# High and low parts of seven half rows of y moved into the staging tile of the output weights, at 14 address offsets

## The chip, the cores and the metric

The kernel runs on one core of a Trainium2 chip. A core has five engines with a queue each: TensorE (PE in the profile; its weight loads are shown apart, as PEld), VectorE (DVE), ScalarE (ACT), GpSimd (POOL) and SyncE (SP), which issues most DMAs. The metric is the time of one execution on the device in microseconds, taken as the median of several runs. All memory named below is the core's SBUF, 128 partitions wide; an address or a distance is counted in bytes within a partition.

## The reference

One layer of an encoder on a sequence of 1024 rows and 1024 channels, in float32:

```python
h = rmsnorm(x, norm_mix_w[l]) * (1 + sc_m) + sh_m
z, xbc, dt_raw, q, k, v = jnp.split(h @ w_in[l], IN_SPLITS, axis=-1)
y_ssd = ssd_mixer(z, xbc, dt_raw, ...)      # Mamba-2 scan, 512 columns
y_att = chunk_attention(q, k, v, rel_bias[l])   # 512 columns
x = x + g_m * (jnp.concatenate([y_ssd, y_att], axis=-1) @ w_out[l])
h = rmsnorm(x, norm_ffn_w[l]) * (1 + sc_f) + sh_f
x = x + g_f * conv_ffn(h, w_up[l], ffn_conv_w[l], w_down[l])
return rmsnorm(x, final_norm_w)
```

The change touches the line with `w_out`: y, 1024 by 1024, times the output weights.

## The kernel before

Matmuls are made from a faster float32 format (F32R). Each operand is split into a high part, which is the value rounded to that format, and a low part, the rest; a product is three matmuls: high by high, high by low, low by high. `split` (L88 to L94) does it in two instructions: L93 writes the high part, in the output projection on ScalarE, and L94 writes the low part on VectorE as value minus high part.

The work runs in stages: projections and attention (to about 250 us), the convolution and the z projection (to about 407 us), the scan with the output projection (about 407 to 540 us), the feed-forward up products (a Strassen-like scheme with tiles named uX, uY and uZ) and the down products (dn).

In the scan stage the sequence is cut into eight chunks c of 128 rows. Per chunk the scan computes `ydp`, `yop` and `stp` on TensorE, then on VectorE the sums `yy` (L1005 to L1008), the multiplication by the gate `zs` (L1013), a norm, and a transpose back into the tile `xs` (L1023, on ScalarE). GpSimd does part of the elementwise work. Between these pieces stands the output projection, which fills TensorE: row tile st (128 rows) of y is two half rows, `n = 2 * st + part`. Even n are the attention half, held in the tile `ya`; odd n are the scan's half, in `xs`. `wout_half(n)` (L1048) runs the 24 matmuls of half row n: for two column halves of the result and four blocks of 128 channels, three matmuls each. The y block (128 columns) is the stationary operand, that is, the weight load; the output weights (512 columns), kept in the tiles hH and hL, are the moving operand. The results gather in PSUM tiles named `wops`. When both halves of a row tile are done, `wout_row` adds the residual (L1080, L1081), stores it and computes the norm's sum.

`wout_rhs` (L1043) splits a half row ahead of its use: half row n + 1 is split when half row n begins. The target is the tile `yhl` with the tag `wh` in the pool `wu`: two buffers of 4096 bytes, used in turn, so that a split must wait until the matmuls of the half row that last used the buffer have read it. The same two buffers serve earlier stages, and later the feed-forward tiles `cv`. The remaining half rows, 9 to 15, are split after the scan, among the transposes of the feed-forward input.

`wos` (L690) is a tile of 3 x 1024 floats (12288 bytes) in the pool `bcp`. It stages the adaptive weights and the output weights while they are folded and split (L749, L760, L762); after the z projection it isn't used again. When the scan is over, `bcp` is closed (`es_b.close()`), and tiles of the feed-forward stage are laid over its memory, among them the tiles `a`, which are first written at L1179, and the tile `cg`.

In the kernel's allocation every large tile starts at the same address modulo 512 (448), the output weights and both buffers of `yhl` included. The z weight tiles are the exception: 2 x 288 floats (2304 bytes), two blocks of 1152 bytes, of which 260 floats are used.

The order of the work: on TensorE the instructions of the scan and of half rows up to 8 are tied one behind another by `pe` (L862). A few instructions on the other engines are tied to one another (`issue_after`). All else is placed on its engine by a planner that simulates the program, with the waits for buffers, when the program is built. From half row 14 (TensorE) and row tile 6 (VectorE, ScalarE) on, the order is that of the program's text (recorded under L66).

Of the kernel before, what the change touches and what calls it, by code (L numbers as in the profile page):

```python
# [10 lines left out]
F32 = mybir.dt.float32  # L11
F32R = mybir.dt.float32r
# [4 lines left out]
P = 128  # L17
D = 1024
# [20 lines left out]
XM = (5, 7, 7, 7)  # L39
WARM = (8, 26)  # L40
KH = NF // 2

B_ADA, NMIX, NFFN, SNW, SCW, SCB, FCW, DTB, ALOG, DSK = (
    0, 48, 56, 64, 68, 100, 108, 240, 248, 256)
# [4 lines left out]
def f32(ap):  # L49
    return ap.bitcast(F32)  # L50
# [22 lines left out]
def tile_block(ctx: ExitStack, tc: tile.TileContext, x, ccol, pk, w_ada, w_first, w_ft, w_z,  # L73
               w_out, w_up, w_down, bias, fnw, out, dbg=None):
    nc = tc.nc
    V, A, T = (InOrder(tc, e) for e in (nc.vector, nc.scalar, nc.tensor))
# [11 lines left out]
    def split(hi, lo, src, ehi, elo, scale=None):  # L88
        if scale is not None:
            A.activation(hi, src, AF.Copy, scale=scale)  # L90
            V.scalar_tensor_tensor(lo, src, scale, f32(hi), op0=ALU.mult, op1=ALU.subtract)
            return
        i = A.activation(hi, src, AF.Copy) if ehi is A else ehi.tensor_copy(hi, src)  # L93
        return i, elo.tensor_tensor(lo, src, f32(hi), ALU.subtract)  # L94
# [5 lines left out]
    wu = es_l.enter_context(tc.tile_pool(name="wu", bufs=2, reuse_waits="tile"))  # L100
# [38 lines left out]
    def raw_tile(n=1024):  # L139
        rawc[0] += 1  # L140
        return raws[:, rawc[0] % 2, 0:n]
# [34 lines left out]
    def c4(ap):  # L176
        return ap.rearrange("p (a b) -> p a b", a=4)
# [33 lines left out]
    def mod_shift(dst, sh, kt, n=1):  # L211
        return V.tensor_tensor(dst[:, kt:kt + n], modc[:, sh + kt:sh + kt + n],
                        pkt[:, B_ADA + sh + kt:B_ADA + sh + kt + n], ALU.add)
# [147 lines left out]
    for j in range(2):  # L361
        k = slice(4 * j, 4 * j + 4)
# [43 lines left out]
    for hh in range(2):  # L406
# [13 lines left out]
        for kt in range(KT):  # L420
            if hh == 0:
# [7 lines left out]
                t = raw_tile(768)  # L429
# [194 lines left out]
    def gemm_part(p, which, hhs):  # L624
        if which == 0:
            new_pair(p)
        if which == 2 and hhs == H1:
            wh, wl = held.pop(p)
        elif p == 2 and which < 2:
            with tc.issue_after(wpin[0].ins), tc.issue_after(wpin[1].ins):  # L630
                wh, wl = wu_pair(w_ft[8 + 3 * (p - 2) + which], A, V)
        else:
            wh, wl = wu_pair(w_ft[8 + 3 * (p - 2) + which], A, G)
        if which == 2 and hhs == H0:
            held[p] = wh, wl
        outs = {hh: psv.tile([P, 512], F32, tag="acc", bufs=1, name="acc") for hh in hhs}
        gemm_ft(wh, wl, outs, GPIN.get((p, which, hhs), {}), hhs)
        for hh in hhs:
            tmp = tps = None
            if which == 2:  # L640
                tmp, tps = p_tile()[:, 0:512], tp_tile()
            evac_qkv(p, which, hh, outs[hh], tmp, tps)
# [15 lines left out]
    part = lambda *a: (lambda: gemm_part(*a))  # L658
# [9 lines left out]
    x1 = (ya, xs)  # L668
# [9 lines left out]
    bcp = es_b.enter_context(tc.tile_pool(name="bcp", bufs=1, side="right", reuse_waits="tile"))  # L678
# [8 lines left out]
    tle1 = bcp.tile([P, 2, P], F32, name="tle1")  # L687
    tle, ones = tle1[:, 0, :], tle1[:, 1, :]
    sgt = bcp.tile([P, P], F32, name="sgt")
    wos = bcp.tile([P, 3, D], F32, name="wos")  # L690
    es_t = ExitStack()
    es_g = ExitStack()
    gm1 = es_g.enter_context(tc.tile_pool(name="gmp", bufs=1, side="left")).tile([P, 512], F32, name="gm1")
# [166 lines left out]
    def pe(op, *a, **k):  # L860
        with tc.issue_after(chain[0]) if chain and chain[0] else ExitStack():
            i = op(*a, **k)  # L862
        if chain:
            chain[0] = i.ins
# [161 lines left out]
    x1d = dram.tile([S, D], F32, name="x1d")  # L1026
    NM = (KH + 1) // 2

    def kn(m):
        return min(2, KH - 2 * m)  # L1030

    gd = {}
    for m in range(NM):
        for n, names in (("x", ("b11",)), ("y", ("t1", "t3")), ("z", ("t2", "t4", "b21", "b22"))):
            t = gd[n, m] = dram.tile([kn(m), P, len(names), 512], F32, name=f"g{n}{m}")
# [2 lines left out]

    mod_scale(affn, SC_F, NFFN, 0, KT)
    mod_shift(bffn, SH_F, 0, KT)  # L1040
    xr_, yq, wps, xrs = {}, {}, {}, []

    def wout_rhs(st, part):  # L1043
        if st < NT:
            y = yq[st, part] = wu.tile([P, 2, 4, P], F32R, tag="wh", name="yhl")
            return split(y[:, 0], y[:, 1], x1[part][:, st, :].rearrange("p (a b) -> p a b", a=4), A, V)[1].ins

    def wout_half(n, ks=slice(0, 8), fill=()):  # L1048
        st, part = n // 2, n % 2
        if ks.start == 0:  # L1050
            if part == 0:
                if not xrs:
                    xrs.append(wu.tile([P, 2, 2, 512], F32, tag="w2", bufs=1, name="xr"))
                xr_[st] = xrs[0][:, st % 2]
                nc.sync.dma_start(xr_[st].rearrange("p a b -> p (a b)"), x[st * P:(st + 1) * P, :])
                wps[st] = []
            for q in {0: (0, 2), 1: (), 2: ()}.get(n, (n + 1,)):
                wout_rhs(q // 2, q % 2)
        y = yq[st, part]
        for dh, k in [(dh, k) for dh in range(2) for k in range(4)][ks]:  # L1060
            w = ws[dh][4 * part + k]
            if len(wps[st]) <= dh:
                wps[st].append(ps2a.tile([P, 512], F32, tag="w1", bufs=1, name="wops") if n == 2 and not dh else
                               ps2b.tile([P, 512], F32, tag="wo", bufs=PB[0], name="wops"))
            ps = wps[st][dh]
            f, l = part == 0 and k == 0, part == 1 and k == 3
            pe(T.matmul, ps, y[:, 0, k, :], w[0], start=f, stop=False)
            pe(T.matmul, ps, y[:, 0, k, :], w[1], start=False, stop=False)
            pe(T.matmul, ps, y[:, 1, k, :], w[0], start=False, stop=l)
        if part == 1 and ks.stop == 8:  # L1070
            wout_row(st, *fill)

    def wout_row(st, mid=(), end=()):
        xr = xr_.pop(st)
        m = [stat(), stat()]
        for dh in range(2):
            src = wps[st][dh]
            if dh:
                src = x1[dh][:, st, :]
                V.tensor_tensor(src, wps[st][dh], gm1, ALU.mult)  # L1080
            V.tensor_tensor(xr[:, dh, :], src, xr[:, dh, :], ALU.add)  # L1081
            nc.scalar.dma_start(x1d[st * P:(st + 1) * P, halves[dh]], xr[:, dh, :])
            A.activation(x1[dh][:, st, :], xr[:, dh, :], AF.Square, scale=1.0 / 32.0, accum_out=m[dh])
        for fn in mid:
            fn()
        scale_[:] = [(st, xr, rstd2(m))]
        for fn in end:
            fn()
        if not chain:
            row_scale()  # L1090
# [22 lines left out]
    for c in range(NT):  # L1113
        if c == 1:
            ssd_turn(*turn)
        y, t = ssd_y(c, *pre)
        if c > 1:
            ssd_turn(*turn)
        if c == 1:
            at = wout_rhs(0, 1)  # L1120
        if c == 2:
            wout_half(2, slice(4, 8))
            wout_rhs(1, 1)
        if c > 1:
            ssd_norm(c, y, t)
        turn = (c, y)
        n, k = ((0, slice(0, 3)), (2, slice(0, 4)), (3, slice(0, 3)))[c] if c < 3 else (c + 1, slice(0, 3))
        if c < NT - 1:
            if c == 0:
                ssd_norm(c, y, t)  # L1130
            pre = ssd_pre(c + 1, x_tile, lambda: wout_half(n, k))
            late = pin[1]
            if c == 1:
                ssd_norm(c, y, t, at)
            row_scale(pin[0])
            if c == 1:
                wout_half(1)
            else:
                wout_half(n, slice(3, 8))
        else:  # L1140
            wout_half(c + 1)
# [42 lines left out]
    def a_tile():  # L1184
        return hp.tile([P, 2, S], F32, tag="a", bufs=2, name="a")
# [32 lines left out]
    class Unit:  # L1218
        def __init__(self, i):
            self.i, self.b, self.ps, self.w, self.done = i, (ya, xs)[i // KH], {}, {}, set()  # L1220
            nc.sync.dma_start(self.b[:, 0, :], w_up[i, :, 0, :])
            nc.sync.dma_start(self.b[:, 1:4, :], w_up[i, :, 1:4, :])
# [32 lines left out]
        def post(self, p):  # L1255
# [15 lines left out]
            elif p == "Q4":  # L1271
                V.tensor_tensor(self.v[:, 0:512], ps, self.v[:, 0:512], ALU.subtract)
                self.a = a_tile() if self.i % KH < KH - 1 else \
                    self.b[:, 0:4, :].rearrange("p (a b) c -> p a (b c)", a=2)
# [13 lines left out]
        def finish(self):  # L1288
# [3 lines left out]
            V.tensor_tensor(a[:, 1, :], a[:, 0, :], a[:, 1, :], ALU.mult)  # L1292
            if self.i < KH:
                nc.scalar.dma_start(gd["x", self.i // 2][self.i % 2, :, 0], a[:, 1, 0:512])
# [29 lines left out]
    for sts in ((0, 1), (2, 3)):  # L1324
# [4 lines left out]
        for n in (9,) if sts[0] == 0 else (10, 11):  # L1329
            wout_half(n)  # L1330
    units = [Unit(0), Unit(KH)]
    for u in units:
# [99 lines left out]
    bufs = {}  # L1432
# [317 lines left out]
```

## Time and profile before

| | |
|---|---|
| median of 3 runs | 1180.53 us (1179.7 to 1180.82) |
| the profiled execution | 1180.9 us |
| its span, first to last instruction | 1179.2 us |
| mean granted TensorE clock | 0.997 |
| PE busy | 1154.7 us (98%), 5839 matmuls |
| output projection | 384 matmuls of 512 columns, from 409.7 to 537 us |

In the views, a row such as "L862 PE MATMUL wops<-hH,yhl" names the source line, the engine, the operation and the tiles: written, then read. In a row of the timeline the first two numbers are the start and the duration in us; brackets at the end tell how long the engine sat idle before it and what ended that. In the view of instructions by tile the three numbers are the shortest, the median and the longest duration in ns. Matmuls overlap: one of 512 columns shows 389 ns, while the next one starts 227 ns later; starts tell the pace.

### The profile page before, as it was taken

How to read it: one execution, taken by the hardware profiler on the slowest of the kernel's cores; microseconds unless marked ns; L12 is line 12 of the kernel's file. 1: busy time of each engine (PE TensorE's matmuls, PEld its weight loads, DVE VectorE, ACT ScalarE, POOL GpSimd, SP SyncE). 2: the span in 40 equal slices, each digit the busy share in tenths (PEclk: the TensorE clock that was granted, in tenths of full speed). 3: DMA queues.
4: the chain of work that ended last, by engine and by line, in shares of the span. 5: the costliest groups of instructions: out<-in, count | busy, mean ns of one | idle time of the engine just before them, and what ended most of it. 6: DMA issues, size and time to landing. Idle time of an engine off the chain costs nothing.

```text
span 1179.2 us, 15793 instructions
## 1 busy us (share of the span) xinstructions
PE 1154.7 (98%) x5839; PEld 974.9 (83%) x5839; DVE 907.4 (77%) x1357; ACT 587.9 (50%) x971; POOL 162.2 (14%) x179
## 2 busy tenths in 40 slices
PE   8999999999999999999999999999999999999996
PEld 7778888888889988887788888888888888888885
DVE  7746465787676778558999988898888869666986
ACT  5636464674335665587444454434433445433454
POOL 1103343350000165200000000000000000000622
PEclk9999999999999999999999999999999999999999
DMA  9736344244558622141233222332233378633444
GB/s 349 260 83 158 100 121 125 57 153 128 185 179 294 224 101 81 64 152 36 95 110 134 101 80 95 128 127 75 93 107 116 117 277 301 242 122 121 160 134 152
DMA packets 63741, 169.15 MB, mean 143 GB/s; under 512 B 6880, under 2 KB 7344, under 8 KB 62256
## 3 DMA queue, kind: packets, MB, share of 16 engines
q1 hardware_dynamic: 56320, 143.11, 36.8%
q10 hardware_dynamic: 7344, 25.04, 5.4%
q8 instruction: 46, 0.75, 0.3%
q14 instruction: 31, 0.25, 0.1%
HBM read 125.87 MB, written 32.81 MB: 135 GB/s over the span
## 4 chain that ended last, share of the span: by engine, by line
PE 82%; DVE 11%; ACT 3%; issue 3%; POOL 1%; POOLq 0%; DVEq 0%; ACTq 0%
PE wops L862 5%; PE dn L86 5%; PE dn L84 5%; PE dn L85 5%; PE uY L86 5%; PE uY L84 5%; PE uY L85 5%; PE uX L86 3%; PE uZ L84 3%; PE uZ L85 3%; PE uZ L86 3%; PE uX L84 3%; PE uX L85 3%; PE s L84 3%; PE s L86 3%
## 5 line engine op out<-in xcount | busy, mean ns | idle before, releaser
L85 PE MATMUL dn<-w 128*128 128x512 f32 x296 | 107.4, 389 | 0.0
L84 PE MATMUL dn<-w 128*128 128x512 f32 x296 | 107.4, 389 | 0.0
L86 PE MATMUL dn<-w 128*128 128x512 f32 x296 | 99.9, 390 | 0.1
L84 PE MATMUL uY<-tH,w 128*128 128x512 f32 x248 | 96.5, 389 | 0.0
L86 PE MATMUL uY<-tH,w 128*128 128x512 f32 x248 | 96.5, 389 | 0.0
L85 PE MATMUL uY<-tL,w 128*128 128x512 f32 x248 | 96.5, 389 | 0.0
L1611 POOL TENSOR_TENSOR ya<-ya,xs 128x512 f32<-128x512 f32 x4 | 18.2, 4590 | 551.0 <-ACT xs L1607 551.0
L93 ACT ACTIVATE w<-ya 128x1024 fp32r<-128x1024 f32 (+1 forms) x41 | 39.2, 955 | 85.2 <-PE uY L86 75.2
L862 PE MATMUL wops<-hH,yhl 128*128 128x512 f32 x224 | 73.0, 397 | 0.6 <-DVE yhl L94 0.6
L535 POOL TENSOR_SCALAR p<-p,st 128x640 f32<-128x640 f32 (+4 forms) x64 | 50.2, 794 | 116.4 <-DVE st L534 113.5
L86 PEld LDWEIGHTS dn<-w 128*128 128x128 f32 x296 | 55.4, 188 | 12.6 <-DVE w L94 1.2
L85 PEld LDWEIGHTS dn<-w 128*128 128x128 f32 x296 | 55.6, 188 | 11.6
L84 PEld LDWEIGHTS dn<-w 128*128 128x128 f32 x296 | 55.6, 188 | 11.5
L93 ACT ACTIVATE w<-xs 128x1024 fp32r<-128x1024 f32 (+1 forms) x41 | 39.2, 955 | 37.1 <-PE uY L86 30.9
L529 DVE CUSTOM_DVE_ANT_0 p<-s,bias 128x640 f32<-128x640 f32 (+4 forms) x58 | 38.3, 675 | 23.1 <-PE tp L561 8.8
L86 PEld LDWEIGHTS uY<-tH,w 128*128 128x128 f32 x248 | 46.5, 188 | 9.7
L84 PEld LDWEIGHTS uY<-tH,w 128*128 128x128 f32 x248 | 46.5, 188 | 9.7
L85 PEld LDWEIGHTS uY<-tL,w 128*128 128x128 f32 x248 | 46.6, 188 | 9.6
L532 ACT ACTIVATE p<-p,st 128x640 f32<-128x640 f32 (+4 forms) x64 | 44.1, 692 | 17.9 <-DVE st L529 17.4
L94 DVE TENSOR_TENSOR pt<-tp,pt 128x512 fp32r<-128x512 f32 (+2 forms) x72 | 41.8, 596 | 13.3 <-ACT pt L93 12.9
L1285 DVE SCALAR_TENSOR_TENSOR a<-cv,pkt,a 128x1023 f32<-128x1023 f32 (+1 forms) x40 | 51.1, 1280 | 0.1
L84 PE MATMUL s<-hH,wh 128*128 128x512 f32 x128 | 50.4, 394 | 0.1
(503 smaller groups left out, 3399.3 us busy)
## 6 DMA issues: line engine op xcount, KB each, us to landing
gz<-a ACTq DMA_DIRECT2D x10, 1024.0 KB, 5.1
ya<-in_w_up_dram SPq DMA_DIRECT2D x11, 768.0 KB, 4.2
xs<-in_w_up_dram SPq DMA_DIRECT2D x11, 768.0 KB, 4.2
adat<-in_w_ada_dram SPq DMA_DIRECT2D x16, 512.0 KB, 6.0
xs<-in_w_ada_dram SPq DMA_DIRECT2D x16, 512.0 KB, 4.8
raws<-in_w_ft_dram SPq DMA_DIRECT2D x15, 512.0 KB, 3.7
qk<-qk SPq DMA_DIRECT2D x56, 128.0 KB, 2.4
gy<-a ACTq DMA_DIRECT2D x10, 512.0 KB, 2.6
```

The costliest lines, as they stand in the source:

```text
L84: T.matmul(ps, lh, rh, start=start, stop=False, skip_group_check=more)
L85: T.matmul(ps, lh, rl, start=False, stop=False, skip_group_check=more)
L86: T.matmul(ps, ll, rh, start=False, stop=stop, skip_group_check=more)
L93: i = A.activation(hi, src, AF.Copy) if ehi is A else ehi.tensor_copy(hi, src)
L94: return i, elo.tensor_tensor(lo, src, f32(hi), ALU.subtract)
L529: V.tensor_tensor_reduce(out=dst, in0=src, in1=bsl, scale=-1.0, scalar=3e38, op0=ALU.add, op1=ALU.min, accum_out=nm)
L532: A.activation(pv_, pv_, AF.Exp, scale=-1.0, bias=nm, accum_out=rs)
L535: last_g.append(G.tensor_scalar(pv_, pv_, rr, 1.0, op0=ALU.mult, op1=ALU.mult).ins)
L862: i = op(*a, **k)
L1285: V.scalar_tensor_tensor(a[:, j:S], c[:, 0:S - j], w[2 - j], a[:, j:S], op0=ALU.mult, op1=ALU.add)
L1611: G.tensor_tensor(src, src, fnr[:, halves[1]], ALU.mult)
```

## The change

Seven half rows, n = 1 and 3 to 8, are no longer split into the two `wh` buffers but into a new tile `yhw`, which takes the memory of `wos` (tag "wos", one buffer, 2 x 1536 floats, again 12288 bytes). Its first half serves the even n and its second half the odd n. In each half the high part starts at `YOFF[n][0]` bytes and the low part at 2560 bytes plus `YOFF[n][1]` bytes. 2560 and the half's 6144 are multiples of 512, so these 14 numbers, from 16 to 496, are the distances modulo 512 from the output weights that the matmuls stream. Half rows 0, 2 and 9 to 15 stay in the `wh` buffers, which they now use in another turn. What is computed, and with which instructions, stays the same.

```diff
+YBASE = 0
+YOFF = {1: (256, 224), 3: (32, 288), 4: (192, 16), 5: (480, 240), 6: (320, 352), 7: (96, 416), 8: (160, 496)}
...
-    wos = bcp.tile([P, 3, D], F32, name="wos")
+    wos = bcp.tile([P, 3, D], F32, tag="wos", bufs=1, name="wos")
...
     def wout_rhs(st, part):
         if st < NT:
-            y = yq[st, part] = wu.tile([P, 2, 4, P], F32R, tag="wh", name="yhl")
-            return split(y[:, 0], y[:, 1], x1[part][:, st, :].rearrange("p (a b) -> p a b", a=4), A, V)[1].ins
+            n = 2 * st + part
+            if n in YOFF:
+                if not yh2:
+                    yh2.append(bcp.tile([P, 2, 3 * D // 2], F32R, tag="wos", bufs=1, name="yhw"))
+                t = yh2[0][:, n % 2, :]
+                y = [c4(t[:, o:o + 512]) for o in (YBASE + YOFF[n][0] // 4, YBASE + 640 + YOFF[n][1] // 4)]
+            else:
+                t = wu.tile([P, 2, 4, P], F32R, tag="wh", name="yhl")
+                y = [t[:, 0], t[:, 1]]
+            yq[st, part] = y
+            return split(y[0], y[1], c4(x1[part][:, st, :]), A, V)[1].ins
...
-            pe(T.matmul, ps, y[:, 0, k, :], w[0], start=f, stop=False)
-            pe(T.matmul, ps, y[:, 0, k, :], w[1], start=False, stop=False)
-            pe(T.matmul, ps, y[:, 1, k, :], w[0], start=False, stop=l)
+            pe(T.matmul, ps, y[0][:, k, :], w[0], start=f, stop=False)
+            pe(T.matmul, ps, y[0][:, k, :], w[1], start=False, stop=False)
+            pe(T.matmul, ps, y[1][:, k, :], w[0], start=False, stop=l)
```

More of the change, by code (lines that the diff above doesn't have):

```diff
@@ L1040, in tile_block @@
     mod_shift(bffn, SH_F, 0, KT)
-    xr_, yq, wps, xrs = {}, {}, {}, []
+    xr_, yq, wps, xrs, yh2 = {}, {}, {}, [], []
     def wout_rhs(st, part):
         if st < NT:
-            y = yq[st, part] = wu.tile([P, 2, 4, P], F32R, tag="wh", name="yhl")
-            return split(y[:, 0], y[:, 1], x1[part][:, st, :].rearrange("p (a b) -> p a b", a=4), A, V)[1].ins
+            n = 2 * st + part
[9 more added lines that the diff above has]
+            return split(y[0], y[1], c4(x1[part][:, st, :]), A, V)[1].ins
     def wout_half(n, ks=slice(0, 8), fill=()):
```

## The prediction

> **What bounds the kernel now.** I read the page first, then the busy time by stretches, then the waits of the stage that the change touches, then the chain and the timeline there.
>
> ```profile
> span 1179.2 us, 15793 instructions
> PE 1154.7 (98%) x5839; PEld 974.9 (83%) x5839; DVE 907.4 (77%) x1357; ACT 587.9 (50%) x971; POOL 162.2 (14%) x179
> L862 PE MATMUL wops<-hH,yhl 128*128 128x512 f32 x224 | 73.0, 397 | 0.6 <-DVE yhl L94 0.6
> ```
>
> TensorE is the bound: 98% busy, and the output projection (wops) lost only 0.6 us waiting for a split half row (yhl). Seven of the sixteen half rows move. The stretches of that stage (columns: PE, PEld, DVE, ACT and POOL busy, granted clock, DMA share, GB/s):
>
> ```profile
> 410.00:430.00 20.00, 20.00 (x110) 17.02 (x108) 13.32 (x17) 13.44 (x37) 13.69 (x14) 1.00 0.32 120
> 430.00:450.00 20.00, 19.41 (x106) 16.50 (x105) 17.24 (x23) 13.39 (x33) 11.35 (x12) 1.00 0.33 118
> 450.00:470.00 20.00, 19.74 (x115) 17.09 (x114) 17.10 (x24) 13.02 (x34) 11.22 (x12) 1.00 0.23 80
> 470.00:500.00 30.00, 29.80 (x160) 25.52 (x159) 18.31 (x28) 14.70 (x30) 8.78 (x11) 1.00 0.18 62
> ```
>
> PE is idle for 0 + 0.59 + 0.26 + 0.20 = 1.05 us in these 90 us, at the full clock. All that could be won here without faster matmuls is that 1.05 us. Who waited for whom between 406 and 545 us (total, times, longest):
>
> ```profile
> ACT yhl L93 <- PE wops L862: 0.6, 2, 0.4
> PE wops L862 <- DVE yhl L94: 0.6, 1, 0.6
> PE ydp L862 <- DVE th L908: 0.5, 2, 0.3
> ```
>
> The first row is the whole price of the two staging buffers: a split that has to wait until the matmuls of an older half row have read the buffer. It is 0.6 us, on ACT, not on PE. The second row is the one place where PE waits for a split. Its place in the chain, and on the engines:
>
> ```profile
> 434.73 0.69 DVE yy L1013
> 435.42 1.46 DVE yhl L94
> 436.92 5.28 PE wops L862 x22
> ```
>
> ```profile
> 433.12 0.64 ACT L93 ACTIVATE yhl<-xs 128x512 fp32r<-128x512 f32 x1
> 433.68 1.01 DVE L1008 TENSOR_TENSOR yy<-yy,yt 128x512 f32<-128x512 f32 x1
> 435.34 1.53 DVE L94 TENSOR_TENSOR yhl<-xs,yhl 128x512 fp32r<-128x512 f32 x1
> 436.92 0.73 PE L862 MATMUL wops<-hH,yhl 128*128 128x512 f32 x2 [0.59 <-DVE yhl L94]
> ```
>
> This is half row 3. Its high part is written at 433.12, long before PE needs it; its low part stands in VectorE's queue behind the scan's own work and runs 1.53 us. No buffer is waited for, so a new buffer doesn't take this wait away.
>
> **The change part by part.** Half rows 1 and 3 to 8 are split into the dead 12 KB staging tile instead of the two rotating 4 KB buffers. No instruction is added: each still costs one ACT copy, one DVE subtraction and 24 matmuls, 7 x 24 = 168 matmuls in all, 112 with a high part as weights and 56 with a low one. Five things can differ.
>
> *Pace of the matmuls.* In the kernel before, all operands of the projection start at the same address modulo 512 bytes (the big tiles' starts differ by multiples of 512 in its allocation); now weights and moving operand are 16 to 496 bytes apart. The trace has no such pair in steps of 16. Its nearest rows are those of the z projection: its weight blocks are 1152 bytes apart and its tiles 2304, so against the activations its pairs pass through distances 0, 128, 256 and 384. First and last of 24 of its matmuls, then of nine of the output projection (PE only):
>
> ```profile
> 397.37 0.28 PE L66 MATMUL s<-wzh,hH 128*128 128x260 f32 x1
> 400.13 0.28 PE L66 MATMUL s<-wzh,hL 128*128 128x260 f32 x1
> 440.00 0.39 PE L862 MATMUL wops<-hH,yhl 128*128 128x512 f32 x1
> 441.81 0.39 PE L862 MATMUL wops<-hH,yhl 128*128 128x512 f32 x1
> ```
>
> The first run takes 2.76 us for 23 starts, 120 ns each, through all four distances; the second, at distance 0, 1.81 us for 8 starts, 226 ns. So 252 columns more cost 106 ns, 0.42 ns a column; 512 columns take about 216 ns and some 10 ns are fixed per weight load and matmul. If a distance removed those 10 ns, 168 of them would be 1.7 us less; if it doubled them, 1.7 us more. The far end is a weight load that becomes the bound itself:
>
> ```profile
> L862 PEld LDWEIGHTS wops<-hH,yhl x224: 186/188/192, 409.7 to 523.9; 128*128 128x128 f32 x112
> L66 PEld LDWEIGHTS vps<-wsh,hH x64: 186/192/333, 17.0 to 97.5; 128*128 128x128 f32 x64
> ```
>
> A load is 188 ns and hides behind a matmul of 226; the longest load of the kernel is 333 ns, and 168 x (333 - 226) would be 18.0 us. I take 0: the z rows are the nearest, and their pace is even over four distances.
>
> The Trainium skill, TensorE: Matmul & The Clock Gate, Part 2, says that PE has two independent SBUF read ports, one for the streaming operand and one for the weight load, so that loading the next weights takes nothing from the running matmul; by it no distance matters and this term is 0, which the even 120 ns of the z rows agree with. The same page (section on the 56 ns gap) puts the warm start-to-start time of a 512-column matmul at 215.7 ns, against 226 here; if the new distances brought that pace, it would be an estimated 168 x 10.6 = 1.8 us less.
>
> *Writes at the new addresses.* ACT and DVE write 14 half rows at odd distances. The rows of zs are 2080 bytes apart, so the multiplication by z reads chunk 0 at distance 0 and chunk 7 at 224:
>
> ```profile
> 409.66 0.69 DVE L1013 TENSOR_TENSOR yy<-yy,zs 128x512 f32<-128x512 f32 x1
> 487.89 0.69 DVE L1013 TENSOR_TENSOR yy<-yy,zs 128x512 f32<-128x512 f32 x1
> ```
>
> The same 0.69 us: I cost this at 0. Those are reads; for a write the bound is a whole instruction more or less hidden, and PE's slack of 1.05 us covers one.
>
> *Waits that go.* Half row 10 finds its buffer free since half row 2. Before, it waited for half row 8:
>
> ```profile
> 491.69 0.61 PE L862 MATMUL wops<-hH,yhl 128*128 128x512 f32 x2
> 492.11 0.64 ACT L93 ACTIVATE yhl<-ya 128x512 fp32r<-128x512 f32 x1 [0.20 <-PE wops L862]
> 498.44 0.64 ACT L93 ACTIVATE yhl<-xs 128x512 fp32r<-128x512 f32 x1 [0.40 <-PE wops L862]
> ```
>
> 0.20 us of ACT goes; PE is full there (29.80 of 30), so nothing on the path. Half row 11 still writes over half row 9, so its 0.40 us stays. Half rows 1, 3, 4 and 9 are freed from a buffer too, but none of them shows a wait for one; what they stand behind is ACT's and DVE's own work.
>
> *Waits that come.* The staging tile must have been read for the last time before half row 1 is written, and the feed-forward tiles that are laid over it must now wait for the matmuls of half row 8:
>
> ```profile
> 403.41 1.23 DVE L762 TENSOR_TENSOR hL<-wos,hH 128x1024 fp32r<-128x1024 f32 x1 [0.53 <-ACT hH L760]
> 419.57 0.63 ACT L93 ACTIVATE yhl<-xs 128x512 fp32r<-128x512 f32 x1
> 497.04 1.01 ACT L1179 ACTIVATE a<-xps,bffn,affn 128x256 f32<-128x256 f32 x2
> ```
>
> Last read 404.64 against 419.57: 15 us to spare. Half row 8's last matmul starts by about 491.9, the first write of a tile over it is at 497.04: some 4.5 us to spare. Both 0. Behind that write ACT holds the next split (498.44) and SP no load of this tile, so a miss would be felt on PE only after the 4.5 us are used up. Within the new tile halves alternate, so from half row 5 on each waits for the one two before it, as now.
>
> *The order on the engines.* Only PE's half rows and a few places are tied by hand here; the rest is placed by a planner that simulates the waits. With five splits freed it may place them elsewhere. That is the term I can't cost from a row; the bounds are the gain of the whole 1.05 us of idle PE and, on the other side, the first rival below. I take 0.
>
> Sum: 0 us of change on the profiled execution's 1180.9 us (span 1179.2 and 1.7 around it). That execution lies 0.4 above the median of the runs, 1180.53, so I forecast 1180.5, with its own range 1179.4 (all idle won) to 1182.2 (ten ns more a matmul). 0.2%, 2.4 us, is about what a measurement of this kernel tells from no change, so this is no change.
>
> **The rivals.** *Freed splits pushed in front (slower).* The last matmul of half row 2:
>
> ```profile
> 434.82 0.39 PE L862 MATMUL wops<-hH,yhl 128*128 128x512 f32 x1
> ```
>
> Half row 4 no longer depends on it, so the planner may put its copy and subtraction ahead of the scan's. DVE has no gap there from 433.68 to the end of half row 3's split; one more subtraction, 0.69 us alone or 1.53 as at 435.34, delays that split and with it PE, which already waits. Half rows 9 and 10 could do the same further on. It decides once a split is placed between L1008 and L94 of an earlier half row: three places x 0.69 to 1.53 = 2.1 to 4.6 us, 1182.6 to 1185.1, say 1183.6. Against it: those splits stand in the order in which the program names them, and ACT ran half row 4 only at 439.65, four us after its buffer came free:
>
> ```profile
> 439.65 0.63 ACT L93 ACTIVATE yhl<-ya 128x512 fp32r<-128x512 f32 x1
> ```
>
> *Distances cost pace (slower).* Weight reads and moving reads that collide: 10 ns more each gives 1182.2, several times that 1184 to 1186, the load-bound end 1198. Against it: the even z rows.
>
> *Distances gain pace (faster).* The fixed 10 ns go: 1178.8; with all idle time, 1177.8. For it: the 10 ns are there in every matmul and unexplained. Against it: they are the same at four distances. That the distances do nothing, and the change so shows nothing, is my forecast.
>
> **How the numbers follow.** No change: 0.47. Splits in front: 0.20, of which 0.14 lands beyond 1182.9 and 0.06 within 0.2%. Distances slower: 0.12, of which 0.08 beyond and 0.04 within. Distances faster, with or without idle time: 0.09, of which 0.06 within. A replanned order that tightens what follows 500 us: 0.05, faster. Causes not named: 0.05 faster, 0.02 slower. So slower 0.14 + 0.08 + 0.02 = 0.24, faster 0.03 + 0.05 + 0.05 = 0.13, no change 0.47 + 0.06 + 0.04 + 0.06 = 0.63. The range goes from 1178.0, below the gain of pace, to 1185.1, the end of the first rival; about 0.1 is left out above and 0.08 below.
>
> **What would show it.** Right: starts of the 168 matmuls 226 to 227 ns apart in all seven half rows; 188 ns loads; the 0.59 us wait at half row 3 still there; the 0.20 us wait of half row 10 gone; the first feed-forward write without a wait for PE. Wrong: a pace that differs from half row to half row (then the distance counts, and the offsets say which), loads well over 188 ns, a split of half row 4, 9 or 10 that precedes the scan's DVE work with PE idle behind it, or a wait for PE in front of the first feed-forward write.

## The result and the profile after

The changed kernel takes 1183.84 us (median of 13 runs, 1181.73 to 1185.87) against 1180.82 us before (13 runs beside them, 1178.84 to 1182.18). The ratio is 1.0027, with a 95% interval of 1.0019 to 1.0036: slower by about 3.2 us, where no change was forecast.

The page of the changed kernel:

```profile
span 1181.0 us, 15793 instructions
PE 1153.7 (98%) x5839; PEld 973.3 (82%) x5839; DVE 907.4 (77%) x1357; ACT 587.6 (50%) x971; POOL 162.7 (14%) x179
```

The span of this execution is only 1.8 us longer. It was lucky ahead of the change: the last matmul of the z projection (zps) starts 1.66 us earlier than in the profile before, and the first of the up products (uX) 1.44 us later. Most of the head start, 1.3 us, comes about between 48 and 52 us, where the TensorE clock stood at 0.50 in the profile before and at 1.00 here. So the stage between them lost 3.1 us, about what the medians say. The same stretches as shown of before (PE, PEld, DVE, ACT, POOL busy, clock, DMA share, GB/s):

```profile
410.00:430.00 20.00, 20.00 (x111) 17.29 (x110) 12.40 (x17) 13.45 (x39) 13.31 (x14) 1.00 0.24 87
430.00:450.00 20.00, 19.42 (x104) 16.36 (x103) 16.77 (x22) 12.83 (x31) 11.63 (x12) 1.00 0.33 118
450.00:470.00 20.00, 19.79 (x114) 16.97 (x114) 17.10 (x24) 13.72 (x35) 11.46 (x12) 1.00 0.24 80
470.00:500.00 30.00, 28.44 (x153) 24.05 (x152) 16.66 (x26) 13.19 (x28) 8.88 (x11) 1.00 0.19 63
```

The clock is full in all of them. The first three are as before within 0.05 us of PE busy time; in the last, PE is idle for 1.56 us in place of 0.20. The waits of PE from 404 to 545 us show this one and another that lies just ahead of 410:

```profile
PE ydp L864 <- DVE th L910: 1.8, 2, 1.6
PE xps L864 <- DVE zs L812: 1.2, 1, 1.2
PE wops L864 <- DVE yhw L96: 0.6, 1, 0.6
```

The third is the wait at half row 3 that was there before. The wait for th was 0.5 in all, the one for zs is new. (The lines stand two further down than before: L93 is L95, L862 is L864, L908 is L910.)

**The new wait.** The timeline of the kernel before, and then that of the changed one, where the scan begins:

```profile
407.23 0.76 DVE L810 SCALAR_TENSOR_TENSOR zs<-zs,zps 128x260 f32<-128x260 f32 x2 [1.25 <-ACT zs L809]
409.10 0.61 PE L862 MATMUL xps<-ct,bt 128*128 128x128 f32 x4
```

```profile
405.59 0.63 ACT L95 ACTIVATE yhw<-ya 128x512 fp32r<-128x512 f32 x1
405.73 0.43 DVE L812 SCALAR_TENSOR_TENSOR zs<-zs,zps 128x260 f32<-128x260 f32 x1 [1.25 <-ACT zs L811]
406.25 0.69 DVE L96 TENSOR_TENSOR yhw<-ya,yhw 128x512 fp32r<-128x512 f32 x1
...
408.31 0.41 DVE L812 SCALAR_TENSOR_TENSOR zs<-zs,zps 128x260 f32<-128x260 f32 x1
...
408.78 0.71 PE L864 MATMUL xps<-ct,bt 128*128 128x128 f32 x4 [1.17 <-DVE zs L812]
```

Before, VectorE read the last two pieces of z from PSUM one behind the other (x2). Now the split of half row 4 stands between them, 34 us earlier than its old place (439.65 on ACT): its buffer is free, so the planner puts it in the first gap, where VectorE waits for ScalarE. Two instructions of the scan slip in behind it, and the second piece of z is read at 408.31. xps takes the PSUM bank of that piece, and PE stands still for 1.17 us. Half row 4 isn't multiplied before 446 us.

**The longer wait.** The same on ACT and DVE at half rows 9 and 10, ahead of the multiplication into th:

```profile
467.70 0.63 ACT L95 ACTIVATE yhl<-xs 128x512 fp32r<-128x512 f32 x1
...
468.24 0.61 ACT L95 ACTIVATE yhl<-ya 128x512 fp32r<-128x512 f32 x1
...
471.57 0.68 DVE L96 TENSOR_TENSOR yhl<-xs,yhl 128x512 fp32r<-128x512 f32 x1
...
472.17 1.53 DVE L96 TENSOR_TENSOR yhl<-ya,yhl 128x512 fp32r<-128x512 f32 x1
...
473.62 1.28 DVE L910 TENSOR_TENSOR th<-th,cb 128x512 f32<-128x512 f32 x2
...
474.45 1.97 PE L864 MATMUL ydp<-xdt,th 128*128 128x64 f32 x16 [1.56 <-DVE th L910]
```

Both splits (0.68 + 1.53 us) run before th, which starts at 473.62; PE waits 1.56 us for it, 0.20 before. Half row 10's own 0.20 us wait for a buffer is gone, and PE needs half row 9 only at 493 us. On PE, POOL and SP the order of the instructions is the same in both kernels; on ACT and DVE only these three splits moved.

**The pace.** Two matmuls of half row 3, four rounds of three matmuls apart:

```profile
438.02 0.63 PE L864 MATMUL wops<-hH,yhw 128*128 128x512 f32 x2
...
440.82 0.63 PE L864 MATMUL wops<-hH,yhw 128*128 128x512 f32 x2
```

That is 2.80 us for four rounds (high by high, high by low, low by high), 700 ns each. The rows quoted in the prediction, 440.00 to 441.81 at distance 0, are 8 starts of 226 ns, 680 for a round of three. In steady state the seven half rows show rounds of 693, 700, 688, 699, 693, 693 and 693 ns (n = 1, 3, 4, 5, 6, 7, 8). The loads haven't changed, 188 ns:

```profile
L864 PEld LDWEIGHTS wops<-hH,yhw x112: 186/188/192, 422.2 to 492.9; 128*128 128x128 f32 x112
```

The lag of the changed kernel behind the one before, start against start, adds these up:

```
last zps matmul  -1.66
first xps        -0.32   +1.34  the wait for zs
half row 0       -0.22   +0.10
half row 3       -0.41   -0.19  (its start is set by VectorE; the pace of n = 1 is absorbed here)
half row 6       -0.17   +0.24  pace of n = 3, 4, 5
half row 7       +1.28   +1.45  1.36 wait for th, 0.09 pace of n = 6
first uX         +1.44   +0.16  0.13 pace of n = 7 and 8
```

So by this profile the order on the engines costs 2.7 us and the pace about 0.5. The runs below take the two apart.

### The profile page after: what moved, and what is told of

Same layout as the page of the kernel before. It is cut to its first block, busy times and chain, and to the rows that moved or that the text cites. A ratio compares the mean times of both kernels' runs of the same rounds, so it can differ in the third digit from the quotient of the medians.

```text
span 1181.0 us, 15793 instructions
## 1 busy us (share of the span) xinstructions
PE 1153.7 (98%) x5839; PEld 973.3 (82%) x5839; DVE 907.4 (77%) x1357; ACT 587.6 (50%) x971; POOL 162.7 (14%) x179
## 4 chain that ended last, share of the span: by engine, by line
PE 79%; DVE 12%; ACT 4%; issue 4%; POOL 1%; DMA 0%; POOLq 0%; DVEq 0%; ACTq 0%; SPq 0%
PE dn L88 5%; PE dn L86 5%; PE dn L87 5%; PE wops L864 5%; PE uY L88 5%; PE uY L87 5%; PE uY L86 5%; PE uX L88 3%; PE uZ L87 3%; PE uZ L88 3%; PE uZ L86 3%; PE uX L87 3%; PE uX L86 3%; PE s L86 3%; PE s L88 3%
## 5 line engine op out<-in xcount | busy, mean ns | idle before, releaser
L95 ACT ACTIVATE w<-ya 128x1024 fp32r<-128x1024 f32 (+1 forms) x41 | 39.1, 955 | 85.3 <-PE uY L88 75.2
L95 ACT ACTIVATE w<-xs 128x1024 fp32r<-128x1024 f32 (+1 forms) x41 | 39.1, 954 | 37.0 <-PE uY L88 31.0
L88 PE MATMUL s<-hH,wl 128*128 128x512 f32 x128 | 50.5, 394 | 0.0
```

Of the source, the lines that this page charges most:

```text
L88: T.matmul(ps, ll, rh, start=False, stop=stop, skip_group_check=more)
```

## The experiments

**Distance 0, the new buffers kept.** All 14 offsets are 0, the order is that of the changed kernel.

```diff
-YOFF = {1: (256, 224), 3: (32, 288), 4: (192, 16), 5: (480, 240), 6: (320, 352), 7: (96, 416), 8: (160, 496)}
+YOFF = {1: (0, 0), 3: (0, 0), 4: (0, 0), 5: (0, 0), 6: (0, 0), 7: (0, 0), 8: (0, 0)}
```

> The changed kernel with all 14 offsets 0, so that every operand stands at distance 0 again; buffers and order as in the changed kernel. Theory (order and distances both count): the half rows run at 227 ns a matmul, the early splits of half rows 4, 9 and 10 stay, so about 2.4 us over before (1.2 where PE waits for zs near 408 us, 1.4 where it waits for th near 474 us). Rival, distances alone: 0 over before. Rival, order alone: 3 us over before, as in the changed kernel.

Measured: 1183.37 us (1181.42 to 1186.74, 11 runs) against 1180.42; ratio 1.0019 (1.001 to 1.0028), 2.2 us. (The microseconds beside a ratio are worked out from the ratio; the two medians here lie 2.95 us apart.) Half row 3, and the wait for th, in the timeline:

```profile
439.25 0.62 PE L864 MATMUL wops<-hH,yhw 128*128 128x512 f32 x2
...
441.97 0.62 PE L864 MATMUL wops<-hH,yhw 128*128 128x512 f32 x2
...
475.57 3.04 PE L864 MATMUL ydp<-xdt,th 128*128 128x64 f32 x16 [1.74 <-DVE th L910]
```

2.72 us for four rounds, 680 ns: the pace is back in all seven half rows, and most of the loss stays. So it isn't the distances that cost most. Both waits are there, and the one for th is 1.74 us long (1.56 in the changed kernel).

**The old order, the new distances.** The splits of half rows 4, 9 and 10 are tied behind the instructions that they stood behind before. The order on PE, DVE, POOL and SP is then that of the kernel before; on ACT one copy precedes six small instructions of the next chunk.

```diff
+HOLD = (4, 9, 10)
...
+            at = {4: [rsc.get((0, 1)), rad.get((1, 0))], 9: [rsq.get((3, 0)), rgm.get(3)], 10: gated[0:2]}.get(n, []) if n in HOLD else []
...
-            return split(y[0], y[1], c4(x1[part][:, st, :]), A, V)[1].ins
+            with ExitStack() as es:
+                for i in at:
+                    es.enter_context(tc.issue_after(i))
+                return split(y[0], y[1], c4(x1[part][:, st, :]), A, V)[1].ins
...
-            for q in {0: (0, 2), 1: (), 2: ()}.get(n, (n + 1,)):
+            for q in {0: (0, 2), 1: (), 2: (), 3: ()}.get(n, (n + 1,)):
...
                 wout_half(n, slice(3, 8))
+                if c == 2:
+                    wout_rhs(2, 0)
```

> The changed kernel with its 14 offsets, but the splits of half rows 4, 9 and 10 held behind the instructions behind which they stood before. Theory: both waits of PE go, 3 to 9 ns more a matmul in seven half rows stay, so 0.6 to 0.8 us over before. Rival, distances alone: 3 us over before. Rival, order alone: 0.

Measured: 1180.64 us (1179.48 to 1181.79, 11 runs); ratio 1.0004 (0.9995 to 1.0012). PE's waits in the stage:

```profile
PE ydp L865 <- DVE th L911: 0.2, 1, 0.2
```

The wait for zs is gone and that for th is 0.2 us. The rounds are as slow as in the changed kernel: four of half row 3 take 2.80 us (439.30 to 442.10), 700 ns each.

So the slower pace alone costs about 0.5 us, which the measurement can't tell from nothing, and the order the rest.

**The old order at distance 0.** Both edits together.

> Both undone: splits held and all offsets 0; only the new buffer and its waits are left. Theory: 0 over before, within 0.5 us. If the new memory or its waits cost something by themselves, it stays here.

Measured: 1180.36 us (1179.01 to 1181.4, 11 runs); ratio 0.9998 (0.9989 to 1.0006). The kernel is as fast as before: the new buffers by themselves, the freed ones, and the feed-forward tiles that lie over the new one cost nothing and give nothing that these runs can tell (1.3 us less to 0.7 more). In the profile the stretch from the last zps matmul to the first uX takes as long as before, to 0.01 us. With the two runs above, the loss lies in the order and the distances: 2.2 and 0.5 us, 2.7 of the measured 3.2 (2.2 to 4.2). It is also the best version found, and it doesn't beat the kernel before.

**Half row 4 free alone, distance 0.** `HOLD = (9, 10)`, and half row 4 is split where the changed kernel names it.

> Offsets 0, half rows 9 and 10 held, half row 4 free to go early. Theory: 1.2 us over before, PE waiting for zs near 408 us and not for th near 474 us. If the early start of half row 4 is made up for later, 0.

Measured: 1181.6 us (1179.53 to 1183.23, 11 runs); ratio 1.0007 (0.9998 to 1.0016), 0.8 us, which by itself isn't clear of nothing. Of the two waits only the one for zs is there, and from the last zps matmul to the first uX the profiled execution loses 1.22 us:

```profile
PE xps L865 <- DVE zs L813: 1.2, 1, 1.2
```

**Half rows 9 and 10 free, distance 0.** The reverse, `HOLD = (4,)`.

> Half row 4 is split where it stood before, half rows 9 and 10 where the changed kernel has them; all distances 0. Theory (the order of the engines carries most of the loss, and its two parts add): the wait of PE for zs is gone, the wait of 1.6 to 1.7 us for th at about 474 us stays; the time is that of e1 less that of e4's part, 2.2 - 0.8 = 1.4 us above before, so about 1181.8, and higher still in executions where the granted clock falls behind that wait as it did in the profile of e1 (0.81 and 0.85 there). Rival (the wait for zs is the one that matters and the one for th is taken in again by what follows): within 0.5 us of before, 1180.9 at most.

Measured: 1183.93 us (1181.93 to 1185.83, 6 runs) against 1179.42; ratio 1.0034 (1.0022 to 1.0046), 4.0 us. The rival is out: the wait for th isn't taken in again. But the cost is more than the wait, and the sum of the parts overshoots: 0.8 and 4.0 for the two parts, 2.2 for both together, and the interval of the 4.0 doesn't hold the 1.4 expected. The timeline and then stretches of 1 us behind the wait show what this execution lost besides the wait:

```profile
475.18 2.57 PE L865 MATMUL ydp<-xdt,th 128*128 128x64 f32 x16 [1.74 <-DVE th L911]
```

```profile
476.00:477.00 1.00, 1.00 (x9) 1.00 (x8) 0.25 (x1) 1.00 (x3) 0.00 (x0) 0.68 0.85 344
477.00:478.00 1.00, 1.00 (x5) 0.99 (x5) 0.58 (x2) 0.45 (x2) 0.00 (x0) 0.50 0.24 82
478.00:479.00 1.00, 1.00 (x4) 0.74 (x3) 0.55 (x1) 0.42 (x1) 0.00 (x0) 0.50 0.00 0
479.00:480.00 1.00, 1.00 (x4) 0.80 (x3) 0.40 (x1) 0.00 (x0) 0.00 (x0) 0.61 0.00 0
```

The eighth column is the granted clock. Right behind the wait it falls to one half: 0.32 + 0.50 + 0.50 + 0.39 = 1.71 us of clock is lost, which is 3.4 us at half speed. The first run above (all free, distance 0) had the same in its profile, for twice as long: (0.19 + 0.15) x 10 = 3.4 us lost, 6.8 us at half speed.

```profile
470.00:480.00 10.00, 8.26 (x37) 7.01 (x36) 7.41 (x10) 4.34 (x8) 5.75 (x6) 0.81 0.17 54
480.00:490.00 10.00, 10.00 (x48) 8.47 (x48) 6.06 (x10) 2.71 (x6) 2.46 (x3) 0.85 0.07 26
```

In the changed kernel's own profile the wait is 1.56 us and the clock stays at 1.00. So part of what the last run lost was clock, and it need not apply to the changed kernel.

**A shorter and a longer wait.** Both at distance 0 with half row 4 held: `HOLD = (4, 10)` leaves one subtraction in front of th; a second copy of one VectorE instruction of that chunk, ahead of th, makes the wait longer.

```diff
-HOLD = (4,)
+HOLD = (4, 10)
```

> As e7, but half row 10 is split where it stood before, so one subtraction (0.68 us) stands in front of the multiplication into th instead of two (0.68 + 1.53). Theory (two costs: the wait itself, and a clock that falls to one half for 3.4 us or twice that in those executions where PE sits idle for more than about 1.7 us, half of 3.4): the wait for th is 0.3 to 0.7 us, no execution shows the lower clock, and the time is 0.2 to 0.7 us above before. Rival (any wait in this place costs clock, or the loss of e7 isn't the wait's): some executions at a mean clock of 0.993 and 2 us or more above before.

```diff
-                V.tensor_tensor(cb.rearrange("p (a b) l -> p a b l", a=2),
+                for _ in range(2 if c == 6 else 1):
+                    V.tensor_tensor(cb.rearrange("p (a b) l -> p a b l", a=2),
...
```

> As e7, with one more VectorE instruction of 0.68 us (the multiplication into cb of that chunk done twice) in front of the multiplication into th. Theory (idle for more than half of a stretch of 3.4 us that runs by itself costs 3.4 us or more at half clock): the wait grows from 1.74 to about 2.4 us, the lower clock shows in about 2.4 / 3.4 = 7 of 10 executions against 3 of 6 in e7, and the time is 2.4 - 0.3 = 2.1 us above before where the clock holds and 3.8 to 5.5 where it falls. Rival (the fall of the clock in e1 and e7 came by chance and has nothing to do with the wait's length): as often as in e7 or less, and the median only 0.7 us above that of e7.

Measured: the shorter one 1181.31 us (12 runs, 1179.82 to 1184.48) against 1179.41, ratio 1.0015 (1.0006 to 1.0023), 1.8 us; the longer one 1185.65 us (5 runs, 1184.15 to 1186.47), ratio 1.0049 (1.0037 to 1.0061), 5.8 us. The waits in the two profiles:

```profile
472.07 1.97 PE L865 MATMUL ydp<-xdt,th 128*128 128x64 f32 x16 [1.14 <-DVE th L911]
```

```profile
475.66 1.97 PE L865 MATMUL ydp<-xdt,th 128*128 128x64 f32 x16 [2.48 <-DVE th L912]
```

The shorter one is 1.14 us long, more than the 0.3 to 0.7 expected: one subtraction is enough to be late. Waits of 1.14, 1.74 and 2.48 us go with 1.8, 4.0 and 5.8 us, so the time follows the length of this wait. Each is more than the wait, but in the profiles the wait itself costs no more than its length. From the last zps matmul to the first uX, counted as in the table of lags above, the three profiled executions lose 0.97, 3.23 and 2.32 us: the wait less the 0.20 us that stood there before, and for the wait of 1.74 us also the 1.71 us of clock. Without that clock its part is 1.54 us; with the 1.22 of half row 4 this gives 2.8, beside the 2.7 of both waits in the changed kernel. So in the profiles the parts add up. Beyond them the profiles show only the fallen clock; what else the times hold isn't traced. Of the executions, 1 of 12, 3 of 6 and 4 of 5 have a mean clock of 0.995 or less, in the order that the theory wanted (0, half, 7 in 10). But the profiled execution of the longer one kept its clock through 2.48 us; its time was still 4.7 us above the median before, of which this stage accounts for 2.3. And executions of the kernel before have such mean clocks too at no longer times (0.995 at 1178.97 us), since the start of the kernel enters the mean. So it is shown that the clock can halve behind a wait of 1.74 us; how often it does, and whether it does in the changed kernel, stays open. In its 13 runs the mean clock lies between 0.995 and 0.997.

**Which distances cost.** Two kernels with the old order and seven other distances each, the same for the high and the low part.

```diff
-YOFF = {1: (256, 224), 3: (32, 288), 4: (192, 16), 5: (480, 240), 6: (320, 352), 7: (96, 416), 8: (160, 496)}
+YOFF = {1: (64, 64), 3: (128, 128), 4: (256, 256), 5: (384, 384), 6: (448, 448), 7: (16, 16), 8: (496, 496)}
```

> Splits held as before; high and low part of a half row at the same distance, in half rows 1, 3, 4, 5, 6, 7, 8: 64, 128, 256, 384, 448, 16, 496 bytes. Theory (any distance but 0 costs): three matmuls in a row take 688 to 701 ns in all seven, against 680 at distance 0. Rival (only starts that are not a multiple of 64 bytes cost): 680 at 64, 128, 256, 384 and 448, and more at 16 and 496 alone.

```diff
+YOFF = {1: (32, 32), 3: (480, 480), 4: (48, 48), 5: (464, 464), 6: (8, 8), 7: (272, 272), 8: (192, 192)}
```

> The same with 32, 480, 48, 464, 8, 272, 192 bytes. Theory: 688 to 701 ns in all seven. Rival (only starts off a multiple of 64): 680 at 192 alone. If small distances are as good as 0, 8 stays at 680.

One execution each, 1182.28 and 1180.95 us beside 1180.6: too little to tell times, but enough for the pace. Half rows 4 and 7 of the first kernel (256 and 16 bytes), then of the second (48 and 272):

```profile
450.62 0.61 PE L865 MATMUL wops<-hH,yhw 128*128 128x512 f32 x2
...
452.66 0.61 PE L865 MATMUL wops<-hH,yhw 128*128 128x512 f32 x2
...
480.43 0.62 PE L865 MATMUL wops<-hH,yhw 128*128 128x512 f32 x2
...
483.83 0.62 PE L865 MATMUL wops<-hH,yhw 128*128 128x512 f32 x2
```

```profile
448.65 0.63 PE L865 MATMUL wops<-hH,yhw 128*128 128x512 f32 x2
...
451.45 0.63 PE L865 MATMUL wops<-hH,yhw 128*128 128x512 f32 x2
...
479.16 0.63 PE L865 MATMUL wops<-hH,yhw 128*128 128x512 f32 x2
...
482.66 0.63 PE L865 MATMUL wops<-hH,yhw 128*128 128x512 f32 x2
```

2.04 us for three rounds and 3.40 for five: 680 ns, as at distance 0. 2.80 for four and 3.50 for five: 700 ns. All fourteen, as the mean of a round of three in steady state:

```
distance, bytes     round of three, ns
0, 16, 256          680
192, 448, 496       684 to 687
8                   692
128, 384            690 to 706, mean 698
32, 48, 64          700
272, 464, 480       700
```

Neither theory holds: 256 and 16 cost nothing, so it isn't every distance; 64, 128 and 384 cost as much as 32 and 48. No distance is faster than 0. I have no rule that gives this table. Each distance but 0 was seen in one half row; that the half row isn't the cause is shown by distance 0, at which all seven hold 680.

**The rest of the kernel at a distance.** The tiles hH and hL, which hold the output weights here and whose memory feeds other stages too, are moved by 32 bytes (a pad of 8 floats ahead of them), and the seven half rows sit at offset 32, so that they are at distance 0 again. The order is held. The other matmuls of 512 columns that pair with these tiles, 2136 by count, are now at 480.

```diff
+    htp.tile([P, 8], F32, name="hpad")
...
+YOFF = {1: (32, 32), 3: (32, 32), 4: (32, 32), 5: (32, 32), 6: (32, 32), 7: (32, 32), 8: (32, 32)}
```

> Splits held; the tiles hH and hL (output weights, activations of the projections and of the feed-forward up products) start 32 bytes later, and the seven half rows start at offset 32 too, so that these 168 matmuls are at distance 0 again, while 2136 other matmuls of 512 columns (acc, s, uY, the half of uZ that reads tH and tL, the other half rows) come to distance 480. Theory (distance counts): the seven half rows back to 680 ns for three matmuls, the others slower by 3 to 7 ns each, 6 to 15 us over before. Rival (the start address of the weights counts, not the distance): the seven half rows slow as with offset 32, the others at 227 ns, 0.5 us over before.

Measured: 1191.14 us (1190.34 to 1191.62, 4 runs) against 1180.6; ratio 1.0088 (1.0071 to 1.0105), 10.4 us. Half row 3 at offset 32, which had 700 ns in the other kernel:

```profile
440.57 0.62 PE L866 MATMUL wops<-hH,yhw 128*128 128x512 f32 x2
...
443.29 0.62 PE L866 MATMUL wops<-hH,yhw 128*128 128x512 f32 x2
```

2.72 us for four rounds, 680. So the distance between the two operands counts, not where the weights start. Half rows 0, 2 and 9 to 15, left where they were, now take 698 to 703. An up product (uY), first before and then here, as the first and last of a run of starts:

```profile
600.13 0.39 PE L84 MATMUL uY<-tH,w 128*128 128x512 f32 x1
...
604.89 0.39 PE L84 MATMUL uY<-tH,w 128*128 128x512 f32 x1
```

```profile
603.01 0.40 PE L87 MATMUL uY<-tH,w 128*128 128x512 f32 x1
...
605.82 0.39 PE L87 MATMUL uY<-tH,w 128*128 128x512 f32 x1
```

4.76 us for 21 starts is 227 ns each, 2.81 for 12 is 234. 2136 matmuls at some 5 to 7 ns are 10.7 to 15 us, and 10.4 came out, 7.4 of it in the up products: the distance of 480 costs outside the output projection too, and against it this kernel's habit of starting all large tiles at one address modulo 512 is worth about 1%.

## Why the prediction was wrong

The forecast was no change, 1180.5; it came out as the first rival said, at 1183.6 there and 1183.84 here, inside the range.

*The order on the engines, taken as 0: wrong.* This is the step that failed. The prediction named it as the one term without a row, and gave the rival that splits would be pushed in front 0.20. The rival had the mechanism and the size (2.1 to 4.6 us; by the profile 1.34 + 1.36 = 2.7), and it named half rows 4, 9 and 10, but it put the delay in the wrong place: it costed three splits ahead of an earlier split, and half row 3's wait stayed at 0.6. They went ahead of the scan's own work, the reading of z and the multiplication into th, where three splits made two waits of PE. That the rival's 1183.6 lies so close to 1183.84 is in part luck, since the measured time holds about 0.5 us of pace that the rival left out. The argument against it, that ACT ran half row 4 four microseconds after its buffer came free, says only that nothing urgent called for it then; it doesn't bind a planner that finds a gap 34 us earlier. With the old order held the loss is 0.5 us with the distances and 0 without, each within about 1 us.

*The pace, taken as 0: wrong in its argument, small in its effect.* Rounds of three take 8 to 20 ns more than 680 (8 x (13 + 20 + 8 + 19 + 13 + 13 + 13) = 0.8 us if every one were steady, 0.5 to 0.6 as it shows at the end of the stage). The even rows of the z projection misled: a 260-column matmul starts every 120 ns at four distances, but two of those, 128 and 384, cost 18 ns a round at 512 columns. So an even pace of the narrow matmuls says little of the wide ones; what sets the pace of either wasn't tested. From the Trainium skill, TensorE: Matmul & The Clock Gate, Part 2, the prediction took two independent SBUF read ports and concluded that no distance matters. The page has no rule on the distance of addresses, and the conclusion doesn't agree with these runs: 10.4 us from a shift of 32 bytes. By what mechanism a distance costs, the runs don't show. The rival of a gain in pace fell as well: no distance was below 680 ns, and the page's 215.7 ns was not reached.

*Weight loads, writes at the new addresses: right.* Loads stay at 186/188/192 ns, the copies at 0.61 to 0.64 us and undisturbed subtractions at 0.68 to 0.69.

*Waits that go and come: right.* Half row 10's 0.20 us is gone, half row 11's 0.40 stays, the 0.59 of half row 3 is 0.58, and the first feed-forward write waits for nothing:

```profile
498.47 1.02 ACT L1190 ACTIVATE a<-xps,bffn,affn 128x256 f32<-128x256 f32 x2
499.88 0.63 ACT L95 ACTIVATE yhl<-xs 128x512 fp32r<-128x512 f32 x1 [0.40 <-PE wops L864]
```

What the prediction left out of "waits that go" is that a wait which never shows can still hold an instruction in its place. Half rows 4 and 9 showed no wait for a buffer, but the buffer kept the planner from putting them early. This last is inferred: the splits move in the same way at distance 0, so the distances aren't the reason, but no run takes back the buffer of one split alone.

## What to carry to other kernels

A buffer that is too busy also orders the work: before you free one, ask where a scheduler will now put the instruction, and who stands behind it on its in-order engine; then hold it in its old place and measure both. Weights and moving operand are best kept at a distance that has been measured for the same shape; in this kernel none was better than the same address modulo 512. A row at another shape is no evidence on a pace unless the same thing sets the pace there.

## What the runs showed of the hardware

The pace of F32R matmuls of 512 columns depends on the address distance, modulo 512, of weights and moving operand: 227 ns at 0, 16 and 256 bytes, up to 233 at others, with no order that I can name. At distance 0 too, half rows 11 and 13 show rounds of 684 to 698 ns in most of these kernels, so something else has a like effect; what it is stays open.

The clock of TensorE fell to 0.50 behind an idle stretch of 1.74 us, for 3.4 us once and 6.8 once, and didn't behind 1.14, 1.56 and 2.48 us, one execution each. But the length of one wait isn't what decides. The kernel before has a fall as well, behind a wait of only 1.40 us at 46.3 us, and in all twelve profiles the changes of the clock within one execution lie whole multiples of 3.41 us apart. Here are four such stretches of 3.41 us (columns as above): the one with that wait and the next, then in the kernel with the longer wait the one in which most of it lies, and the next:

```profile
45.18:48.59 3.41, 1.84 (x13) 1.35 (x11) 2.68 (x7) 2.54 (x5) 1.64 (x1) 1.00 0.44 161
48.59:52.00 3.41, 3.01 (x14) 2.90 (x14) 1.35 (x3) 3.41 (x7) 0.55 (x1) 0.50 0.43 154
```

```profile
471.50:474.91 3.41, 1.68 (x8) 1.06 (x6) 3.38 (x5) 1.96 (x5) 3.28 (x5) 1.00 0.00 0
474.91:478.32 3.41, 2.66 (x20) 2.62 (x21) 2.48 (x4) 2.49 (x4) 0.00 (x0) 1.00 0.59 159
```

The wait of 2.48 us runs across the border at 474.91, 1.74 us on one side and the rest on the other. Leaving out the first 8 and the last 15 us of each execution, the twelve profiles hold nine falls from 1.00. In the stretch ahead of a fall PE was idle for 1.57 to 1.95 us in all. Where no fall followed, it was idle for at most 1.56 us, but for the 1.74 us above. So about half a stretch (1.71 us) divides the two, with 1.57 (a fall) and 1.74 (none) on the wrong side; the ends of matmuls are modelled in a profile, which blurs these figures. Why two of the falls last twice as long stays open.

The Trainium skill, TensorE: Matmul & The Clock Gate, Part 1, describes a free-running window of 3413 ns and a clock of 4/8 or 8/8. These profiles agree with both. For the fall back to half it names at least one idle window (about 3.4 us); here 1.57 to 1.95 us of idle time within one were enough.
